# Third chunk's weights split in the opening, values and keys in the scheduler's order, two conditioning vectors summed in the merge, read-back ring dealt anew

## The chip, the cores and the metric

The kernel runs on one core of a Trainium2 chip. The metric is device time in microseconds for one execution of the whole kernel; the kernel before has a median of 1706.3 us over 3 runs (1700.95 to 1707.58). A profile shows the engines apart: PE multiplies matrices, DVE and POOL do elementwise work with two inputs, ACT does activations and copies, and SP issues every DMA, in the order of its own queue. An engine executes its instructions strictly in program order, so one that waits holds all that stand behind it.

## What is computed

One layer of a diffusion transformer on 512 latent tokens and 256 context tokens of width 1024, in single precision. Cut to what matters:

```python
ml = adaln(c, w_mod, b_mod)          # 9 vectors m0..m8 of 1024 for the latents
mc = adaln(c_ctx, w_mod, b_mod)      # and for the context
h  = ffn_sublayer(x,   ml[0:3], ...) # h + 0.5*gate*norm(swiglu(modulate(norm(h), shift, scale)))
hc = ffn_sublayer(ctx, mc[0:3], ...)
xmc = modulate(rms_norm(hc, g), mc[3], mc[4]);  k_c, v_c = split_kv(xmc @ w_in[:, K_OFF:B_OFF])
xm  = modulate(rms_norm(h, g), ml[3], ml[4])
y   = token_mixer(xm @ w_in, k_c, v_c, ...)   # attention branch + short convolution, gated merge, w_o
h   = h + ml[5] * rms_norm(y, g2)
h   = ffn_sublayer(h, ml[6:9], ...)  # second feed-forward block
```

## The kernel before

**How a product is made.** Each matrix operand is split into a high part (a cast to fp32r, `hi`, line 61, on ACT) and a low part (the difference, `lo`, line 67, mostly on DVE). A product is three PE matmuls: high by high, high by low, low by high. A weight block (a unit, 128x1024, 512 KB) comes by one DMA into one of 4 buffers `wraw`, is split into one of 4 buffers each of `whi` and `wlo` (`unit` and `split`, lines 75 to 88), and a buffer is free again when its last reader is through. With `pool_share` 3, every third low part goes to POOL.

**Who sets the order.** Inside `in_order()` (line 91) PE, DVE, ACT and POOL execute in the order in which the code is written. Outside it a scheduler sets the order of each engine, from costs of its own. The DMA queue, SP, is always put in order by the scheduler.

**The stages,** by the time of the profile:
- Opening, to 90 us (line 511): the shift and scale for the first block from `wmod` (`mod_mm` on PE, `mod_col` to DVE, line 345), the normalised input tiles x0 to x7 (`mod_x`, line 365), and the first two of 22 feed-forward chunks on PE, one k after the other (`open_steps`). `mod_t` (line 389) makes differences of a pair of x tiles on POOL, `mod_tp` splits them. The third chunk's weights need sums of their own: `w_pool` (two operations on POOL), `w_dve` (two on DVE), and the splits `w_hi` and `w_lo`.
- Chunks 2 to 21 of gate and up, to 390 us; the hidden rows go to DRAM (`hl_dram`, `hc_dram`).
- Down projection of the latents to 525 us and of the context to 602 us (`down`, line 758), reading the hidden rows back into a ring of 2 buffers `h` in one pool and 2 `h2` in another. Conditioning vectors 2 to 8 are summed on the way: `mod_acc` (line 559) loads a 512 KB block `mraw` of the weights `wmodr` and adds its rows, scaled, into `macc` on DVE (one instruction L572 and seven L575 per half vector); `mod_sum` (line 579) adds over the partitions with two PE matmuls, copies a row out, and sends it through DRAM to a column. Under the context's part of the down projection the latents' `sandwich` (line 1292: rms norm, gate, residual, second norm, modulation into the operand tiles `xs`) runs step by step, one or two steps per chunk (`take(chain, ...)`).
- Values and keys, 602 to 757 us: `values(q, ts)` (line 854) makes a quarter of the values' columns for latent token blocks 2 to 5 and context blocks 0 and 1, `kv_ctx_k(j)` (line 842) a block of the context's keys. The context's `sandwich` has to be through before the context's part. All of it is inside `in_order()`, with the next two units loaded ahead (`next_unit`), with steps of the context's chain between (`take(steps, ...)`), and then with `late_mods`: vectors 6 and 7, which the second feed-forward block needs.
- Attention and convolution to 1083 us, the merge to 1267 us (`pre`, `post`, `onorm`, lines 1119 to 1183: 32 units, eight times gate, convolution, gate and attention projection; `onorm` normalises the attention's output, which `post(0)` needs whole), w_o, the latents' second sandwich, and the second feed-forward block to the end.

Of the kernel before, what the change touches and what calls it, by code (L numbers as in the profile page):

```python
# [16 lines left out]
P = 128  # L17
DM = 1024
ND = 8
NT = 512  # L20
# [19 lines left out]
class Builder:  # L40
    def __init__(self, tc, ctx, io):
        self.tc = tc
        self.nc = tc.nc
        self.ctx = ctx
        self.io = io
        self.n = 0
        self.nu = 0
        self.pool_share = 0
        self.spaced = False

    def pool(self, stack, name, space=None):
# [73 lines left out]
    def rstd_steps(self, pool, psp, tags, sq, T):  # L125
        nc = self.nc
        nb = T // P
        pst = self.t(psp, [P, 512], tags[0], bufs=tags[1])
        for b in range(nb):
            self.mm(pst[:, b:b + 1], sq[0][:, b * P:(b + 1) * P], self.ones[:, 0:1], True, True)  # L130
        if self.spaced:
            yield
        r = self.t(pool, [P, 8], "rstd_s", bufs=2)
        nc.scalar.activation(r[:, :nb], pst[:, :nb], AF.Sqrt, bias=self.eps, scale=1.0 / DM)
        nc.vector.reciprocal(out=r[:, 4:4 + nb], in_=r[:, :nb])
        yield
        if not self.spaced:
            yield
        pb = self.t(psp, [P, 512], tags[0], bufs=tags[1])
        dgs = []  # L140
        for b in range(nb):
            dg = self.t(pool, [P, P], "rstd_d", bufs=4 if self.spaced else 2)
            nc.vector.tensor_scalar(out=dg, in0=self.ident, scalar1=r[:, 4 + b:5 + b],
                                    scalar2=None, op0=ALU.mult)
# [48 lines left out]
    def build(self):  # L193
# [195 lines left out]
        def mod_t(p):  # L389

            x1, x2 = xt[2 * p], xt[2 * p + 1]
            a, b = slice(0, HK), slice(HK, NKEY)
            u = self.t(sp, [P, 2, HK], "sqt", bufs=2)
            v = self.t(sp, [P, 2, HK], "sqt", bufs=2)
            tt = nc.gpsimd.tensor_tensor
            tt(out=u[:, 0, :], in0=x1[:, b], in1=x1[:, a], op=ALU.subtract)
            tt(out=u[:, 1, :], in0=x2[:, b], in1=u[:, 0, :], op=ALU.subtract)
            tt(out=v[:, 0, :], in0=x2[:, b], in1=x1[:, b], op=ALU.subtract)
            tt(out=v[:, 1, :], in0=x2[:, a], in1=u[:, 1, :], op=ALU.subtract)
            tsum[p] = u, v  # L400
# [110 lines left out]
        with self.in_order():  # L511
# [10 lines left out]
            for i in range(4):  # L522
                next(first)
                if i < 3:
                    mod_col(i + 1, rows.pop(i + 1))
                    mod_x(2 * i + 2)
                    mod_x(2 * i + 3)
                mod_tp(i)
                if i < 3:
                    mod_t(i + 1)  # L530
                if i == 2:
                    w_load(2)
                    w_pool(2)
                    w_hi(2, 0)
                    w_lo(2, 0)
                next(first)
                if i < 2:
                    rows[i + 2] = mod_mm(i + 2)
            w_dve(2)
            w_hi(2, 2)  # L540
            w_lo(2, 2)
        ps0 = result(first)
# [14 lines left out]
        accs = {}  # L557

        def mod_acc(pool, m, q, vs, bufs):
# [19 lines left out]
        def mod_sum(pool, psp, tag, pbufs, m, q, v):  # L579

            acc = accs.pop((m, q, v))
            al = self.t(pool, [P, 2, 512], "mraw", F32R, bufs=2)
            self.hi(al[:, 0], acc)
# [45 lines left out]

        def mod_pipe(jobs, pool, tag):  # L630

            when = {}
            for n, (m, q, v) in enumerate(jobs):
                g = mod_sum(pool, psf, tag, 1, m, q, v)
                for part, at in enumerate((0, 2, 4, 6, 10)):
                    when.setdefault(2 * n + at, []).append((-part, g))
# [107 lines left out]
        psf = self.pool(st, "down_ps", PSUM)  # L744
        fp = self.pool(st, "ffn1")
        xs = [slot(d, [P, 2, NT], F32R) for d in range(ND)]
        xhi, xlo = [t[:, 0, :] for t in xs], [t[:, 1, :] for t in xs]
# [4 lines left out]

        def mod_late(jobs):
            for m, vs, bufs in jobs:
                for q in range(2):
                    yield from mod_acc(fp, m, q, vs, bufs)

        def down(src, n, pre, share):
# [26 lines left out]
        pl = [self.t(psf, [P, 512], f"b{d}") for d in range(ND)]  # L785
        mods = mod_late(((4, (0, 1), 4), (5, (0,), None), (8, (0,), None)))
        inorder = ExitStack()
# [20 lines left out]
        sums = mod_pipe([(4, 0, 0), (4, 1, 0), (4, 0, 1), (4, 1, 1), (5, 0, 0), (5, 1, 0), (8, 0, 0),  # L808
                         (8, 1, 0)], fp, "b4")
# [5 lines left out]
        units = (io["wv"][q, hf] for qs in (range(4), range(3)) for q in qs for hf in range(2))  # L815
        units = iter(list(units) + [io["wk"][j] for j in range(NH)])
        self.pool_share = 3
        ready = [self.unit(next(units)) for _ in range(2)]

        def next_unit():  # L820
            src = next(units, None)
            if src is not None:
                ready.append(self.unit(src))
            return ready.pop(0)
# [8 lines left out]
        drain(chain)  # L833
        xc = [self.t(fp, [P, 2, NCX], f"xc{d}", F32R) for d in range(ND)]
        xchi, xclo = [t[:, 0, :] for t in xc], [t[:, 1, :] for t in xc]
        cx = lambda k: (xchi[k], xclo[k])

        chain = self.sandwich(fp, psf, ("b5", 1), yc, sqyc, gp1c, io["ctxT"], smc, mcx[:, 24:32],
                              xchi, xclo, NCX, None, lambda d: ("rctx", 4), share=False)


        def kv_ctx_k(j):
            w = next_unit()
            pk = self.t(psf, [P, 512], f"b{j % 2 * 3}")
# [9 lines left out]
        def values(q, ts):  # L854
# [32 lines left out]
        steps = chain  # L887
        for q in range(3):
            values(q, [2, 3, 4, 5])
            take(steps, 5)  # L890
        drain(chain)
        steps = late_mods()
        values(3, [0, 1, 2, 3, 4, 5])
        take(steps, 6)
        for q in range(3):
            values(q, [0, 1])
            take(steps, 4)
        for j in range(NH):
            kv_ctx_k(j)
            take(steps, 4)  # L900
        drain(steps)
        inorder.close()
        self.spaced = False
        self.pool_share = 0
        st.close()
# [233 lines left out]
        def onorm():  # L1139
            pst = self.t(mps, [P, 512], "pc", bufs=2)  # L1140
            for h in range(NH):
                sq = self.t(mp, [P, NT], "of", bufs=3)
                nc.sync.dma_start(out=sq, in_=o_dram[h])
# [7 lines left out]
                self.mm(pst, eh, sl, False, h == NH - 1)  # L1151
            r = self.t(mp, [P, NT], "of", bufs=3)
            rh = self.t(mp, [P, NT], "osh", F32R, bufs=1)
# [9 lines left out]
            for h in range(NH):  # L1163
# [5 lines left out]
                self.mm(pr, sel, rl, False, True)  # L1169
                of = self.t(mp, [P, NT], "of", bufs=3)  # L1170
                nc.sync.dma_start(out=of, in_=o_dram[h])
# [167 lines left out]
def take(g, n):  # L1339
    for _ in range(n):  # L1340
        next(g, None)
# [105 lines left out]
```

## Time and profile before

| what | us |
|---|---|
| median of 3 runs (1700.95, 1706.3, 1707.58) | 1706.3 |
| the profiled execution's own time | 1708.63 |
| its span, first to last instruction | 1706.5 |
| PE busy | 1598.8 (94%) |
| DVE busy | 1063.6 (62%) |
| ACT busy | 727.7 (43%) |
| POOL busy | 276.3 (16%) |
| idle of PE, longest single waits | 14.1, 10.3, 8.7, 8.1, 6.5, 6.1 |

How to read it: 2.1 us of the profiled execution lie outside the span, and it is 2.3 us above the median. PE is busy nearly all the time, so time can only be won where PE waits, where its clock is below full (the rows give the granted clock as a share of full speed), or by giving it less to do. A row of the waits names the instruction that waited, by engine and line, and the one whose end released it; a row of the windows gives each engine's busy time in a stretch.

### The profile page before, as it was taken

The numbers are of one execution on the slowest core, as the hardware profiler recorded it, in microseconds if no ns is written. First come the engines' busy times: TensorE is split into PE (matmuls) and PEld (weight loads), VectorE is DVE, ScalarE is ACT, GpSimd is POOL, SyncE is SP. The second block draws the span as 40 slices with busy tenths as digits, with TensorE's granted clock in tenths as the row PEclk, the third lists the DMA queues.
The fourth block names the chain that finished last, engine by engine and source line by source line (L and its number), as shares of the span: only waits on it lengthen the run. The fifth ranks groups of instructions, "written<-read, shape, count | busy, mean of one in ns | idle before, by whom it ended". The sixth has DMA issues, their size and how long they took to land. (4 is left out here: it accounts for less than half of the span.)

```text
span 1706.5 us, 23519 instructions
## 1 busy us (share of the span) xinstructions
PE 1598.8 (94%) x8962; PEld 1425.7 (84%) x8962; DVE 1063.6 (62%) x1463; ACT 727.7 (43%) x1139; POOL 276.3 (16%) x208
## 2 busy tenths in 40 slices
PE   5989999998999878599999999999999999999996
PEld 4889999997889878587888888878889998888886
DVE  4598998865656664647877777473347844333345
ACT  4445444442115442244655556452236732222234
POOL 2433444430002430111010000000002100000003
PEclk9989999999999988789999999999999999999998
DMA  9044444447986844868554653643246753233321
GB/s 365 32 154 167 151 158 151 129 157 265 328 310 199 267 130 148 267 213 230 157 155 139 178 145 108 211 152 102 97 134 199 241 150 117 83 111 93 90 81 50
DMA packets 135704, 282.20 MB, mean 165 GB/s; under 512 B 22932, under 2 KB 61972, under 8 KB 135592
## 3 DMA queue, kind: packets, MB, share of 16 engines
q1 hardware_dynamic: 135592, 280.71, 51.2%
q8 instruction: 70, 1.15, 0.3%
q14 instruction: 42, 0.34, 0.1%
HBM read 229.76 MB, written 38.31 MB: 157 GB/s over the span
## 5 line engine op out<-in xcount | busy, mean ns | idle before, releaser
L63 ACT CAST whi<-wraw 128x1024 fp32r<-128x1024 f32 (+1 forms) x264 | 270.9, 1030 | 476.2 <-PE b L781 100.0
L68 DVE TENSOR_TENSOR wlo<-wraw,whi 128x1024 fp32r<-128x1024 f32 (+1 forms) x249 | 331.9, 1335 | 186.1 <-ACT whi L63 181.7
L108 PE MATMUL f<-xs,whi 128*128 128x512 f32 x640 | 201.7, 394 | 0.9 <-DVE rq L926 0.8
L108 PE MATMUL pa<-xs,whi 128*128 128x512 f32 (+1 forms) x704 | 195.8, 361 | 0.7 <-ACT ob L1043 0.5
L781 PE MATMUL b<-h,whi 128*128 128x512 f32 (+1 forms) x704 | 175.3, 341 | 6.5 <-DMA h<-hl_dram 6.5
L108 PEld LDWEIGHTS pa<-xs,whi 128*128 128x128 f32 x704 | 126.0, 189 | 21.0 <-ACT ob L1043 0.7
L781 PEld LDWEIGHTS b<-h,whi 128*128 128x128 f32 x704 | 123.3, 193 | 21.8 <-DMA h<-hl_dram 6.9
L108 PEld LDWEIGHTS f<-xs,whi 128*128 128x128 f32 x640 | 118.1, 188 | 24.6 <-issue 1.7
L108 PE MATMUL pa<-xs,wlo 128*128 128x512 f32 (+1 forms) x352 | 126.9, 361 | 1.5 <-DVE wlo L68 1.5
L108 PE MATMUL f<-xs,wlo 128*128 128x512 f32 x320 | 125.0, 391 | 0.0
L781 PE MATMUL b<-h,wlo 128*128 128x512 f32 (+1 forms) x352 | 119.4, 339 | 0.1
L108 PE MATMUL pb<-xs,whi 128*128 128x512 f32 (+1 forms) x448 | 114.4, 344 | 0.0
L575 DVE SCALAR_TENSOR_TENSOR macc<-mraw,sc,macc 128x512 f32<-128x512 f32 x112 | 95.8, 894 | 10.0 <-DMA mraw<-wmodr 9.4
L108 PEld LDWEIGHTS pb<-xs,whi 128*128 128x128 f32 x448 | 78.1, 189 | 10.0
L172 POOL TENSOR_TENSOR sqacc<-sqacc,sqt 128x256 f32<-128x256 f32 (+1 forms) x20 | 19.0, 950 | 378.4 <-ACT sqt L170 377.0
L108 PE MATMUL pb<-xs,wlo 128*128 128x512 f32 (+1 forms) x224 | 77.1, 344 | 0.0
L108 PEld LDWEIGHTS pa<-xs,wlo 128*128 128x128 f32 x352 | 66.5, 189 | 11.7 <-DVE wlo L68 1.7
L68 POOL TENSOR_TENSOR wlo<-wraw,whi 128x1024 fp32r<-128x1024 f32 x15 | 37.7, 2516 | 231.7 <-ACT whi L63 231.7
L781 PEld LDWEIGHTS b<-h,wlo 128*128 128x128 f32 x352 | 67.7, 192 | 7.4 <-DVE wlo L68 0.3
L1011 ACT ACTIVATE e<-s,mx 128x768 f32<-128x768 f32 x64 | 57.2, 899 | 34.3 <-DVE mx L1007 34.2
L108 PEld LDWEIGHTS f<-xs,wlo 128*128 128x128 f32 x320 | 60.1, 188 | 12.7
L924 POOL TENSOR_TENSOR rot<-rot,cossin 128x512 f32<-128x512 f32 x16 | 22.2, 1390 | 249.7 <-DVE rot L923 231.1
(355 smaller groups left out, 3632.5 us busy)
## 6 DMA issues: line engine op xcount, KB each, us to landing
mraw<-wmodr SPq DMA_DIRECT2D x56, 512.0 KB
wraw<-f2gu SPq DMA_DIRECT2D x56, 512.0 KB
wraw<-f1gu SPq DMA_DIRECT2D x44, 512.0 KB
wraw<-f1d SPq DMA_DIRECT2D x44, 512.0 KB
hl_dram<-h SPq DMA_DIRECT2D x22, 512.0 KB
h<-hl_dram SPq DMA_DIRECT2D x22, 512.0 KB
wraw<-f2d SPq DMA_DIRECT2D x24, 384.0 KB
wm<-wmod SPq DMA_DIRECT2D x16, 512.0 KB
```

The source lines that it names most:

```text
L63: self.nc.scalar.copy(out=out, in_=src)
L68: (eng or self.nc.vector).tensor_tensor(out=out, in0=src, in1=hi.bitcast(F32), op=ALU.subtract)
L108: self.nc.tensor.matmul(out, lhsT=lhsT, rhs=rhs, start=start, stop=stop)
L172: eng.tensor_tensor(out=a, in0=a, in1=s, op=ALU.add)
L575: nc.vector.scalar_tensor_tensor(out=acc, in0=raw[:, k], scalar=s, in1=acc, op0=ALU.mult, op1=ALU.add)
L781: nc.tensor.matmul(o, lhsT=wt[:, c], rhs=x[:, hl], start=start and f + j == 0, stop=f == NF - 1 and j == 2, skip_group_check=True)
L924: nc.gpsimd.tensor_tensor(out=rt, in0=rt, in1=cs[:, 1, :], op=ALU.mult)
L1011: nc.scalar.activation(e[m], ps[:, m * NKEY:(m + 1) * NKEY], AF.Exp, scale=SCALE, bias=mx[:, 2 + m:3 + m], accum_out=mx[:, 4 + m:5 + m])
```

## The change

What it does, part by part:

1. **Opening.** The third chunk's loads, sums and splits stand in round i = 1 of the loop and no longer in round i = 2 and behind the loop. The last `mod_t` (p = 3) runs on DVE and writes over two tiles that are no longer read.
2. **Read-back ring.** Of the hidden rows' buffers, chunk f takes one of pool `h` for f % 4 in (0, 3), and one of `h2` otherwise; before, (0, 1) took `h`.
3. **Context's down projection.** The latents' chain advances 1 and 2 steps in turn; the four later parts of a sum stand at 2, 3, 5, 9 and no longer at 2, 4, 6, 10.
4. **Values and keys.** `in_order()` ends before the context's sandwich, so that the scheduler orders what follows; the sandwich's statistics use PSUM bank b4, and no longer b5; units are loaded where they are used; `late_mods` is gone from here.
5. **Merge.** Vectors 6 and 7 are summed here, 8 steps after each `post(d)`, with one `mraw` buffer (before, two), two `macc` and PSUM bank pd; the ring `of` of `onorm` has 2 buffers, before 3.

The core of the diff:

```diff
-            u = self.t(sp, [P, 2, HK], "sqt", bufs=2)
-            v = self.t(sp, [P, 2, HK], "sqt", bufs=2)
-            tt = nc.gpsimd.tensor_tensor
+            if p < 3:
+                u, v = (self.t(sp, [P, 2, HK], "sqt", bufs=2) for _ in range(2))
+            else:
+                u, v = (self.t(sp, [P, 2, HK], tag) for tag in ("sqacc", "pbs"))
+            tt = (nc.gpsimd if p < 3 else nc.vector).tensor_tensor
...
-                if i == 2:
+                next(first)
+                if i < 2:
+                    rows[i + 2] = mod_mm(i + 2)
+                if i == 1:
                     w_load(2)
                     w_pool(2)
                     w_hi(2, 0)
                     w_lo(2, 0)
-                next(first)
-                if i < 2:
-                    rows[i + 2] = mod_mm(i + 2)
-            w_dve(2)
-            w_hi(2, 2)
-            w_lo(2, 2)
+                    w_dve(2)
+                    w_hi(2, 2)
+                    w_lo(2, 2)
...
-                raw = self.t(pool, [P, 2, 512], "mraw", bufs=2)
+                raw = self.t(pool, [P, 2, 512], "mraw", bufs=n_mraw[0])
...
-                for part, at in enumerate((0, 2, 4, 6, 10)):
+                for part, at in enumerate((0, 2, 3, 5, 9)):
...
-                pool, tag, bufs = (hp, "h", 2) if f % 4 < 2 else (fp, "h2", 2)
+                pool, tag, bufs = (hp, "h", 2) if f % 4 in (0, 3) else (fp, "h2", 2)
...
-            take(chain, 1 if f < 15 else 2)
+            take(chain, 1 + f % 2)
             take(sums, 1)
...
-        ready = [self.unit(next(units)) for _ in range(2)]
...
         drain(sums)
         drain(chain)
+        inorder.close()
...
-        chain = self.sandwich(fp, psf, ("b5", 1), yc, sqyc, gp1c, io["ctxT"], smc, mcx[:, 24:32],
+        chain = self.sandwich(fp, psf, ("b4", 1), yc, sqyc, gp1c, io["ctxT"], smc, mcx[:, 24:32],
...
-                whi, wlo = next_unit()
-                take(steps, 2)
+                whi, wlo = self.unit(io["wv"][q, hf])
...
-        def late_mods():
-            yield from mod_late(((6, (0,), 4), (7, (0,), 4)))
-            yield from mod_pipe([(m, q, 0) for m in (6, 7) for q in range(2)], fp, "b4")
...
-            take(steps, 5)
+            take(chain, 9)
         drain(chain)
...
-                sq = self.t(mp, [P, NT], "of", bufs=3)
+                sq = self.t(mp, [P, NT], "of", bufs=2)
...
+        def merge_mods():
+            for m in (6, 7):
+                yield from mod_late(mp, ((m, (0,), 2),))
+                yield from mod_pipe([(m, 0, 0), (m, 1, 0)], mp, "pd", 2)
+
+        n_mraw[0] = 1
+        mods = merge_mods()
         pre(0)
         onorm()
         pre(1)
         for d in range(ND):
             post(d)
+            take(mods, 8)
             if d + 2 < ND:
                 pre(d + 2)
+        drain(mods)
```

What this moves on the engines, at three places. In the rows, line numbers are each kernel's own, and the numbers behind a name are a buffer's. First DVE in the opening, around the scale and shift of x6 (`mst` and `s_27`, then `xs_50`, which is x6). Before:

```order
L68 TENSOR_TENSOR xs_127_537<-sqt_413,xs_126_536 128x768
L68 TENSOR_TENSOR wm_539<-sqt_414,wm_538 128x768
L355 TENSOR_TENSOR mst_114<-pd_641,vec_66 128x2 x4
L359 SCALAR_TENSOR_TENSOR s_27_115<-mst_114,vec_66 128x2 x2
L369 SCALAR_TENSOR_TENSOR xs_50_144<-xs_50_144,s_27_115,pbs_249 128x512
L68 TENSOR_TENSOR xe_35_123<-xs_50_144,xe_34_122 128x384
```

And now, with the third chunk's sums `s` and low parts `wlx`:

```order
L69 TENSOR_TENSOR xs_127_537<-sqt_413,xs_126_536 128x768
L69 TENSOR_TENSOR wm_539<-sqt_414,wm_538 128x768
L69 TENSOR_TENSOR wlx_614<-wraw_605,whx_613 128x1024
L470 TENSOR_TENSOR s_136_609<-s_136_609,wraw_605 128x512
L471 TENSOR_TENSOR s_137_610<-wraw_605,s_136_609 128x512
L69 TENSOR_TENSOR wlx_620<-s_136_609,whx_619 128x1024
L356 TENSOR_TENSOR mst_114<-pd_659,vec_66 128x2 x4
L360 SCALAR_TENSOR_TENSOR s_27_115<-mst_114,vec_66 128x2 x2
L370 SCALAR_TENSOR_TENSOR xs_50_144<-xs_50_144,s_27_115,pbs_249 128x512
L69 TENSOR_TENSOR xe_35_123<-xs_50_144,xe_34_122 128x384
```

Four instructions stand ahead of x6's scale that stood behind x7's differences; the second, `s_136`, reads what POOL writes.

Second PE at the end of the context's down projection, where the context's statistics begin (`ones` by `sqacc`); `xs` are the latents' operand tiles, and `h` is a chunk of the hidden rows. Before:

```order
L781 MATMUL b_782_4597<-h_5380,whi_5384 128x256 x2
L781 MATMUL b_782_4597<-h_5380,wlo_5385 128x256
L108 MATMUL b_950_5575<-ones_73,sqacc_0_634_3715 128x1 x2
L872 MATMUL b_937_5551<-whi_5491,xs_610_3691 128x256
L872 MATMUL b_937_5551<-wlo_5492,xs_610_3691 128x256
```

And now, with the last rows of the first quarter of the values ahead of the statistics and the first of the second quarter behind:

```order
L869 MATMUL b_932_5540<-whi_5597,xs_617_3698 128x256 x2
L869 MATMUL b_932_5540<-wlo_5598,xs_617_3698 128x256
L869 MATMUL b_932_5540<-whi_5597,xs_617_3698 128x256
L109 MATMUL b_949_5675<-ones_73,sqacc_0_634_3715 128x1 x2
L869 MATMUL b_960_5716<-whi_5720,xs_610_3691 128x256
L869 MATMUL b_960_5716<-wlo_5721,xs_610_3691 128x256
```

The statistics stood directly behind the down projection and ahead of all values; now a whole quarter of the latents' values stands between.

Third DVE in the merge, while `onorm` squares the attention's output (`osl` is the low part of a head's square) and the branches' weights are split (`wlo`). Before:

```order
L68 TENSOR_TENSOR osl_10104<-of_10101,osh_10103 128x512
L68 TENSOR_TENSOR osl_10113<-of_10110,osh_10112 128x512
L68 TENSOR_TENSOR osl_10122<-of_10119,osh_10121 128x512
L1125 TENSOR_TENSOR cv_10308<-sb_10275,pb_10283 128x512
L68 TENSOR_TENSOR wlo_10414<-wraw_10411,whi_10413 128x1024
L68 TENSOR_TENSOR osl_10131<-of_10128,osh_10130 128x512
```

And now:

```order
L69 TENSOR_TENSOR osl_10017<-of_10014,osh_10016 128x512
L580 SCALAR_TENSOR_TENSOR macc_10273<-mraw_10278,sc_80,macc_10273 128x512
L69 TENSOR_TENSOR wlo_10359<-wraw_10356,whi_10358 128x1024
L69 TENSOR_TENSOR osl_10026<-of_10023,osh_10025 128x512
L580 SCALAR_TENSOR_TENSOR macc_10273<-mraw_10282,sc_80,macc_10273 128x512
L69 TENSOR_TENSOR osl_10035<-of_10032,osh_10034 128x512
L580 SCALAR_TENSOR_TENSOR macc_10273<-mraw_10282,sc_80,macc_10273 128x512
L69 TENSOR_TENSOR wlo_10392<-wraw_10389,whi_10391 128x1024
```

Sums of vector 6 stand between the low parts of the heads and of the weights. Over this stretch, up to the low part of the last head's normalised output, DVE has 16 of these sums, and PE has 299 matmuls of the merge ahead of the first `post`, where before it had 251.

More of the change, by code (lines that the diff above doesn't have):

```diff
@@ L49, in __init__ @@
         self.spaced = False
+        self.n_dg = 2
     def pool(self, stack, name, space=None):
@@ L141, in rstd_steps @@
         for b in range(nb):
-            dg = self.t(pool, [P, P], "rstd_d", bufs=4 if self.spaced else 2)
+            dg = self.t(pool, [P, P], "rstd_d", bufs=self.n_dg)
             nc.vector.tensor_scalar(out=dg, in0=self.ident, scalar1=r[:, 4 + b:5 + b],
@@ L557, in build @@
         accs = {}
+        n_mraw = [2]
         def mod_acc(pool, m, q, vs, bufs):
@@ L581, in mod_sum @@
             acc = accs.pop((m, q, v))
-            al = self.t(pool, [P, 2, 512], "mraw", F32R, bufs=2)
+            al = self.t(pool, [P, 2, 512], "mraw", F32R, bufs=n_mraw[0])
             self.hi(al[:, 0], acc)
@@ L628, in mod_early, with mod_pipe @@
                     ends.extend(sums)
-        def mod_pipe(jobs, pool, tag):
+        def mod_pipe(jobs, pool, tag, bufs):
             when = {}
             for n, (m, q, v) in enumerate(jobs):
-                g = mod_sum(pool, psf, tag, 1, m, q, v)
-                for part, at in enumerate((0, 2, 4, 6, 10)):
+                g = mod_sum(pool, psf, tag, bufs, m, q, v)
+                for part, at in enumerate((0, 2, 3, 5, 9)):
                     when.setdefault(2 * n + at, []).append((-part, g))
@@ L745, in build @@
         fp = self.pool(st, "ffn1")
+        self.n_dg = 4
         xs = [slot(d, [P, 2, NT], F32R) for d in range(ND)]
@@ L751, in build, with mod_late @@
         sqyc, sqyl = self.sqsum(fp, NCX), self.sqsum(fp, NT)
-        def mod_late(jobs):
+        def mod_late(pool, jobs):
             for m, vs, bufs in jobs:
                 for q in range(2):
-                    yield from mod_acc(fp, m, q, vs, bufs)
+                    yield from mod_acc(pool, m, q, vs, bufs)
         def down(src, n, pre, share):
@@ L785, in build @@
         pl = [self.t(psf, [P, 512], f"b{d}") for d in range(ND)]
-        mods = mod_late(((4, (0, 1), 4), (5, (0,), None), (8, (0,), None)))
+        mods = mod_late(fp, ((4, (0, 1), 4), (5, (0,), None), (8, (0,), None)))
         inorder = ExitStack()
@@ L808, in build @@
         sums = mod_pipe([(4, 0, 0), (4, 1, 0), (4, 0, 1), (4, 1, 1), (5, 0, 0), (5, 1, 0), (8, 0, 0),
-                         (8, 1, 0)], fp, "b4")
+                         (8, 1, 0)], fp, "b4", 1)
         self.spaced = True
@@ L812, in build @@
         for f, _ in enumerate(part):
-            take(chain, 1 if f < 15 else 2)
+            take(chain, 1 + f % 2)
             take(sums, 1)
-        units = (io["wv"][q, hf] for qs in (range(4), range(3)) for q in qs for hf in range(2))
-        units = iter(list(units) + [io["wk"][j] for j in range(NH)])
         self.pool_share = 3
-        ready = [self.unit(next(units)) for _ in range(2)]
[L820 to L824, printed above, removed]
         for d in range(ND):
@@ L833, in build @@
         drain(chain)
+        inorder.close()
+        self.spaced = False
         xc = [self.t(fp, [P, 2, NCX], f"xc{d}", F32R) for d in range(ND)]
@@ L836, in build @@
         cx = lambda k: (xchi[k], xclo[k])
-        chain = self.sandwich(fp, psf, ("b5", 1), yc, sqyc, gp1c, io["ctxT"], smc, mcx[:, 24:32],
+        chain = self.sandwich(fp, psf, ("b4", 1), yc, sqyc, gp1c, io["ctxT"], smc, mcx[:, 24:32],
                               xchi, xclo, NCX, None, lambda d: ("rctx", 4), share=False)
         def kv_ctx_k(j):
-            w = next_unit()
+            w = self.unit(io["wk"][j])
             pk = self.t(psf, [P, 512], f"b{j % 2 * 3}")
@@ L881, in values @@
                               .rearrange("t p n -> p t n"), vh[:, hl])
-        def late_mods():
-            yield from mod_late(((6, (0,), 4), (7, (0,), 4)))
-            yield from mod_pipe([(m, q, 0) for m in (6, 7) for q in range(2)], fp, "b4")
-        steps = chain
         for q in range(3):
             values(q, [2, 3, 4, 5])
-            take(steps, 5)
+            take(chain, 9)
         drain(chain)
-        steps = late_mods()
         values(3, [0, 1, 2, 3, 4, 5])
-        take(steps, 6)
         for q in range(3):
             values(q, [0, 1])
-            take(steps, 4)
         for j in range(NH):
             kv_ctx_k(j)
[L900 to L904, printed above, removed]
+        self.pool_share, self.n_dg = 0, 2
         st.close()
@@ L1151, in onorm @@
                 self.mm(pst, eh, sl, False, h == NH - 1)
-            r = self.t(mp, [P, NT], "of", bufs=3)
+            r = self.t(mp, [P, NT], "of", bufs=2)
             rh = self.t(mp, [P, NT], "osh", F32R, bufs=1)
@@ L1169, in onorm @@
                 self.mm(pr, sel, rl, False, True)
-                of = self.t(mp, [P, NT], "of", bufs=3)
+                of = self.t(mp, [P, NT], "of", bufs=2)
                 nc.sync.dma_start(out=of, in_=o_dram[h])
```

## The prediction

> **What bounds the kernel now.** I read the page first, for the engine that sets the time:
>
> ```profile
> span 1706.5 us, 23519 instructions
> PE 1598.8 (94%) x8962; PEld 1425.7 (84%) x8962; DVE 1063.6 (62%) x1463; ACT 727.7 (43%) x1139; POOL 276.3 (16%) x208
> ```
>
> PE is idle for 1706.5 - 1598.8 = 107.7 us. The waits of PE say where; I kept the rows that lie in stages that the change touches (the engine, the line and tile that waited, what released it, the total, how often, the longest):
>
> ```profile
> PE b L872 <- DVE wlo L68: 11.3, 2, 6.1
> PE b L108 <- DVE tmp L178: 10.3, 1, 10.3
> PE b L108 <- ACT mraw L63: 8.7, 1, 8.7
> PE pa L663 <- ACT g L645: 8.1, 1, 8.1
> PE b L108 <- ACT macc L591: 6.6, 4, 4.4
> PE b L781 <- DMA h<-hl_dram: 6.5, 1, 6.5
> PE b L108 <- DVE sqacc L172: 4.7, 2, 2.9
> PE b L108 <- DVE rstd_d L143: 2.8, 1, 2.8
> ```
>
> Then the windows, to see how much each stage loses and at which clock. The columns are the stretch, its length, each engine's busy time with its instructions, PE's granted clock, the DMA engines' busy share and GB/s:
>
> ```profile
> 602.00:641.00 39.00, 26.52 (x200) 26.34 (x200) 23.37 (x43) 15.79 (x32) 12.46 (x11) 0.82 0.39 129
> 641.00:680.00 39.00, 33.97 (x252) 33.53 (x253) 17.82 (x31) 10.35 (x17) 2.94 (x1) 0.87 0.38 130
> 680.00:719.00 39.00, 24.44 (x166) 23.83 (x164) 23.89 (x30) 8.02 (x10) 4.76 (x2) 0.82 0.85 276
> 719.00:757.00 38.00, 28.80 (x181) 26.30 (x182) 19.93 (x29) 16.17 (x25) 4.77 (x2) 0.78 0.60 181
> 622.00:638.00 16.00, 16.00 (x136) 16.00 (x135) 10.44 (x17) 5.29 (x11) 6.39 (x6) 1.00 0.40 132
> 641.00:649.00 8.00, 4.65 (x24) 4.62 (x25) 3.77 (x7) 2.14 (x3) 0.00 (x0) 0.57 0.60 195
> 1083.00:1142.00 59.00, 58.36 (x252) 45.84 (x250) 31.60 (x47) 29.57 (x42) 0.00 (x0) 1.00 0.69 234
> ```
>
> Values and keys, 602 to 757 us, are the worst stage: in 155 us PE is busy for 26.52 + 33.97 + 24.44 + 28.80 = 113.7 us, so 41.3 us idle, and it is busy at a clock of 0.78 to 0.87, while the quiet stretch 622 to 638 has 1.00. The merge's first 59 us lose nothing.
>
> **Values and keys.** What has to be done there is in the groups of PE between 602 and 757 us (shape and count, then busy and mean ns):
>
> ```profile
> L872 PE MATMUL b<-whi,xs 128*128 128x256 f32 x256 | 51.7, 298 | 0.0
> L872 PE MATMUL b<-wlo,xs 128*128 128x256 f32 x128 | 37.9, 296 | 0.0
> L872 PE MATMUL b<-whi,xc 128*128 128x256 f32 x128 | 28.9, 317 | 1.7 <-ACT xc L183 1.1 <-DVE xc L184 0.6
> L108 PE MATMUL b<-xc,whi 128*128 128x256 f32 x128 | 26.4, 307 | 0.3 <-DVE kch L68 0.3
> L872 PE MATMUL b<-wlo,xc 128*128 128x256 f32 x64 | 20.6, 322 | 11.3 <-DVE wlo L68 11.3
> L108 PE MATMUL b<-xc,wlo 128*128 128x256 f32 x64 | 19.5, 305 | 0.0
> L108 PE MATMUL b<-mraw,ones_r 128*128 128x512 f32 x8 | 4.5, 632 | 12.2 <-ACT mraw L63 8.7 <-ACT macc L591 2.3 <-DVE mraw L68 1.2
> ```
>
> Matmuls overlap, so their mean is not their price; the price is the quiet stretch's, 16.00 / 136 = 0.118 us each, and I take 0.12 because a record or two overlap the stretch's ends. There are 256 + 128 + 128 + 128 + 64 + 64 = 768, so 92 us. The two statistics and their spreading are some 16 small matmuls, which I put at 4 us, and what remains at the edges at 1. The stage's work is thus 97 us of its 155; 58 us are loss, and the eight matmuls of the sums leave with it.
>
> How much of the loss goes? The 10.3 us stand at 612 us: PE has nothing but the context's statistics to do there, and their bank b5 is still read by the latents' last modulation on DVE. The change puts a whole quarter of the values, 96 matmuls or 11.5 us, ahead of the statistics, and takes another bank, so PE has work from the first moment; its operands `xs` are then due at the end of the down projection, and the chain that makes them runs at one and a half steps per chunk, so I count them ready. The 11.3 and the 8.7 us are both due to vectors 6 and 7, for DVE is held by their loads, with the weights' low parts queued behind:
>
> ```profile
> DVE macc L575 <- DMA mraw<-wmodr: 9.4, 8, 2.1
> DVE macc L572 <- DMA mraw<-wmodr: 3.6, 2, 1.9
> ```
>
> They leave the stage altogether. What is late next is the context's own chain: two statistics and two spreadings, of which this trace shows waits of 2.9 and 2.8 us. In the new order a quarter stands in front of each statistic, and some 13 matmuls (1.6 us) between it and its spreading. I bound what is left by 0, if all is covered, and by four waits of 2.9 us or 11.6 us, and take 4, nearer the covered end because each chain step now has 11.5 us of PE's work ahead of it. Weights come in 22 units of 512 KB in 97 us, 119 GB/s, and the values go out beside them; the stage moved 276 GB/s in its third window, so I count them as hidden; were they not, see the second rival. The stage takes 97 + 4 = 101 us: **54 us won** (58 to 43, the latter with 11.6 us of waits and their clock).
>
> The clock belongs to that price. Between 641 and 649 us two waits of 2.9 and 2.8 us went with a clock of 0.57. [...]
>
> **The context's down projection.** Of the 6.6 us for `macc` most is one wait of 4.4 us, in which ACT came late with a sum's row copy because it stood behind a weight's load:
>
> ```profile
> 564.26 1.04 ACT L63 CAST whi<-wraw 128x1024 fp32r<-128x1024 f32 x1 [8.94 <-DMA wraw<-f1d]
> 565.75 0.56 ACT L591 COPY macc<-b 1x512 f32<-1x512 f32 x1
> ```
>
> The load itself was issued late, since SP's queue stood behind a write of the latents' chain. In the new spacing each row copy stands one chunk sooner, and the chain's steps lie otherwise, so that a write holds another load, or none in need. I expect 3 us to go, between 0 (the same load is held again) and 7 (all of the 6.6 goes).
>
> **The read-back ring.** The first read of the latents' down projection waits 6.5 us for its hidden rows. The second buffer comes from the other pool, so that its load need not wait for the last spill. The queue at that place (start and length):
>
> ```profile
> 398.34 1.52 SPq L73 DMA_DIRECT2D h<-hl_dram  x3
> ```
>
> The load moves up by a place or two among issues of some 0.5 us, and shares the DMA engines with fewer others: **2 us** of the 6.5, between 0 and 6.5.
>
> **The opening.** These are the rows of DVE, POOL, ACT and PE on which it turns (start, duration):
>
> ```profile
> 67.95 1.46 DVE L369 SCALAR_TENSOR_TENSOR xs<-xs,s,pbs 128x512 f32<-128x512 f32 x1
> 71.72 0.55 DVE L68 TENSOR_TENSOR h<-xs,h 128x384 fp32r<-128x384 f32 x1
> 77.70 2.03 DVE L68 TENSOR_TENSOR wlx<-wraw,whx 128x1024 fp32r<-128x1024 f32 x1
> 86.42 0.68 DVE L467 TENSOR_TENSOR s<-s,wraw 128x512 f32<-128x512 f32 x1
> 67.86 1.01 POOL L399 TENSOR_TENSOR sqt<-xs,sqt 128x384 f32<-128x384 f32 x1
> 82.48 1.27 POOL L461 TENSOR_TENSOR s<-wraw 128x512 f32<-128x512 f32 x1
> 89.50 0.60 ACT L645 ACTIVATE g<-pa 128x512 f32<-128x512 f32 x1
> 72.10 0.34 PE L156 MATMUL pa<-xe,whi 128*128 128x384 f32 x1
> 90.14 1.01 PE L663 MATMUL pa<-xe,whx 128*128 128x384 f32 x2 [8.12 <-ACT g L645]
> ```
>
> x6 is scaled from 67.95, its last low part ends at 72.27, and PE takes it at 72.10: just in time. Now POOL's sum stands behind the third `mod_t`, which ends at 68.87, and ends at 68.87 + 1.27 = 70.1; DVE waits for it, then makes two sums (0.68 each, 71.5), then, after a cast, a low part of 2.0, and so reaches x6 near 74. x6 comes some 6 us later than before: a new stall of 6 us ahead of k = 6, and about 2 us of slow clock behind it. The end of the opening's matmuls moves from 82.0 (90.14 - 8.12) to 90. For that the 8.1 us ahead of the third chunk go, since its splits are done; only a Silu of 0.6 us and its table are left, and PE starts that chunk at about 91 instead of 90.1, but no longer at the half speed that followed the 8.1 us, worth 2.5. **1.5 us won**; if x6 is late by 2 us only, 6 are won, and if by 8, with twice the slow clock, 3 are lost.
>
> **The merge.** Here the vectors arrive again: 32 sums on DVE, 16 loads, 8 matmuls.
>
> ```profile
> L575 DVE SCALAR_TENSOR_TENSOR macc<-mraw,sc,macc 128x512 f32<-128x512 f32 x112 | 95.8, 894 | 10.0 <-DMA mraw<-wmodr 9.4
> 1104.00:1146.00 42.00, 41.82 (x179) 32.23 (x178) 30.02 (x40) 25.26 (x38) 0.00 (x0) 1.00 0.52 165
> ```
>
> The matmuls cost 8 x 58.36 / 252 = 1.9 us. The tight place is `post(0)`, which needs all heads normalised; from 1104 to 1146 us DVE is busy for 30.0 of 42 us with that. Sixteen of the sums now lie in this stretch, 16 x 0.894 = 14.3 us, so 44.3; with a single `mraw` buffer each of the eight loads may hold DVE, by (9.4 + 3.6) / 10 = 1.3 us each as in the rows above, 10.4 us: 54.7 us. For this the scheduler puts 48 more matmuls ahead of `post(0)`, 48 x 0.23 = 11.1 us, so that DVE has 53.1 us. A stall of 2 us by this sum, between 0 and 16 (if the idle time of before can't be filled); I take 4, since SP's loads for `onorm` queue behind those of `mraw`. Sums 17 to 32 lie where DVE has ample idle time. **6 us lost** (2 to 18).
>
> [...]
>
> Between keys and attention a load may come later than now; I count 1 us (0 to 3).
>
> **The sum.** 54 + 3 + 2 + 1.5 - 6 - 1 = 53.5 us. The profiled execution took 1708.6 us, of which 2.1 lie outside its span, and it stands 2.3 us above the median. 1708.6 - 53.5 = 1655, against the median's 1706.3: **1653 us**.
>
> **The rivals.** *The wait moves along with the vectors.* In values and keys the sums cost PE 11.3 + 8.7 us and about 3 of the other sums' waits, with perhaps 7 us of clock, 30 us in all. In the merge there is half the buffering and the same single queue, so the same may happen. Against it: PE has four units in hand there, and the windows show a clock of 1.00. It gives 1653 + 30 - 6 = 1677. *Weights late.* Two units were loaded ahead by hand; the scheduler may load them where they are needed. If each of 22 units costs 1 us, 1675; for it speaks a DMA share of 0.85 in the third window, against it that this window held most of the 16 loads that leave. *Nothing left over.* All chains covered and no stall at `post(0)`: values and keys at 97, the merge at 2, 1645 or less. *No change.* The stage is held by DMA, whatever the order: near 1700; but its first half runs at shares of 0.39 and 0.38 and loses 17.5 us all the same. *Slower.* SP holds a weight behind each `mraw` load, the load waits for DVE, and PE waits for the weight: at half of the 11.3 us for two such waits, 5.65 us, for all 16 loads, 90 us; with the merge at 92 instead of 6 the total is 1653 + 86 = 1739. It is slower than before from 3.7 us per load (59 us in all). Against it: four `wraw` buffers cover several loads.
>
> **How the numbers follow.** The likeliest case, 1653, has a chance of 0.62; the wait that moves along 0.16; late weights 0.10; nothing left over 0.07; slower 0.03; no change 0.02. The bounds of the unknown terms, all good or all bad, would reach from 1632 to 1686; rarely all at once, so for 8 in 10 the range is 1636 to 1680, which holds the likeliest case and most of the next two. A measurement of this kernel tells about 0.5%, 8.5 us, from no change. Faster by more than that: 0.62 + 0.16 + 0.10 + 0.07 = 0.95; within it 0.02; slower 0.03.
>
> **What would show it.** Right: PE's wait on `tmp` L178 gone, values and keys 97 to 112 us long at a clock near 1.00, no `mraw` in their waits; a new wait near 72 us for x6, and no 8 us for `g`; at `post(0)` a wait of a few us for a head's `o`. Wrong: waits on `wlo` or on weights between the quarters; waits on `macc` loads in the merge that add up to 20 us or more; a stage of values and keys above 125 us.

## The result, and the profile after

The changed kernel has a median of 1662.94 us over 4 runs (1660.94 to 1668.42), the kernel before 1705.51 us over 4. The ratio is 0.9759, with a 95% interval of 0.9727 to 0.9791: faster by 2.4%, some 43 us, where 53.5 were forecast. The page's first lines after:

```profile
span 1662.3 us, 23526 instructions
PE 1590.7 (96%) x8962; PEld 1418.7 (85%) x8962; DVE 1061.0 (64%) x1467; ACT 728.4 (44%) x1139; POOL 274.6 (17%) x204
```

The work is the same, 8962 matmuls; PE's idle time fell from 107.7 to 71.6 us. Its waits after (same columns as before; rows of the stages that were changed):

```profile
PE pa L157 <- ACT xe L64: 10.5, 2, 7.0
PE b L787 <- ACT whi L64: 4.6, 1, 4.6
PE b L787 <- DMA h<-hl_dram: 4.3, 1, 4.3
PE b L109 <- DVE sqacc L173: 4.0, 2, 2.0
PE pc L109 <- DVE of L1157: 2.9, 2, 1.7
PE pd L109 <- ACT mraw L64: 2.0, 1, 2.0
PE b L109 <- DVE ml L608: 0.9, 1, 0.9
```

The rows of `tmp`, `wlo` and `mraw` in values and keys, and that of `g`, are gone. New are 7.0 us for x6 (`xe`; the other 3.5 us of its row were there before), and two rows in the merge (`of`, `mraw` to bank pd). The windows of values and keys, and of the merge to and from the first `post`:

```profile
604.00:702.00 98.00, 94.82 (x789) 94.06 (x788) 54.41 (x89) 42.65 (x72) 23.12 (x15) 1.00 0.67 215
1028.00:1104.00 76.00, 70.32 (x298) 55.07 (x298) 45.55 (x65) 31.56 (x44) 0.00 (x0) 0.98 0.76 258
1104.00:1222.00 118.00, 118.00 (x513) 97.22 (x514) 59.87 (x64) 37.02 (x49) 9.89 (x7) 0.98 0.40 125
```

Values and keys have a clock of 1.00 and 3.2 us of idle time; the merge has 5.7 us of idle time ahead of the first `post`, where it had 0.6. From the first and last matmuls of each stage in the two traces:

| stage | before, us | after, us | change | forecast |
|---|---|---|---|---|
| opening and chunks, to the first down projection | 392.5 | 392.7 | +0.2 | -1.5 |
| down projection, latents | 136.5 | 134.8 | -1.7 | -2 |
| down projection, context | 72.8 | 76.6 | +3.8 | -3 |
| values and keys | 154.3 | 97.6 | -56.7 | -54 |
| attention | 327.0 | 326.3 | -0.7 | +1 |
| merge | 183.7 | 193.8 | +10.1 | +6 |
| from w_o to the end | 439.7 | 440.5 | +0.8 | 0 |

The sum is -44.2 us, the difference of the two spans.

### The profile page after: what moved, and what is told of

It reads as the page before. It is cut to its first block, busy times and chain, and to the rows that moved or that the text cites. A ratio compares the mean times of both kernels' runs of the same rounds, so it can differ in the third digit from the quotient of the medians.

```text
span 1662.3 us, 23526 instructions
## 1 busy us (share of the span) xinstructions
PE 1590.7 (96%) x8962; PEld 1418.7 (85%) x8962; DVE 1061.0 (64%) x1467; ACT 728.4 (44%) x1139; POOL 274.6 (17%) x204
## 5 line engine op out<-in xcount | busy, mean ns | idle before, releaser
L69 DVE TENSOR_TENSOR wlo<-wraw,whi 128x1024 fp32r<-128x1024 f32 (+1 forms) x249 | 327.5, 1317 | 181.8 <-ACT whi L64 175.4
L787 PE MATMUL b<-h,whi 128*128 128x512 f32 (+1 forms) x704 | 178.7, 345 | 9.0 <-ACT whi L64 4.6
```

Source lines behind the costliest of these rows:

```text
L69: (eng or self.nc.vector).tensor_tensor(out=out, in0=src, in1=hi.bitcast(F32), op=ALU.subtract)
L787: nc.tensor.matmul(o, lhsT=wt[:, c], rhs=x[:, hl], start=start and f + j == 0, stop=f == NF - 1 and j == 2, skip_group_check=True)
```

## The experiments

Times of stages are from each kernel's own trace, one execution each, between the same matmuls as in the table. The changed kernel is the base unless another is named.

### Values and keys: the vectors or the order

**Vectors 6 and 7 back among values and keys, in the scheduler's order.**

```diff
+        steps = late_mods()
         values(3, [0, 1, 2, 3, 4, 5])
+        take(steps, 10)
...
-            take(mods, 8)
...
-                sq = self.t(mp, [P, NT], "of", bufs=2)
+                sq = self.t(mp, [P, NT], "of", bufs=3)
```

> Vectors 6 and 7 are summed among values and keys again, with two mraw buffers, but in the scheduler's order; the merge is as before, its ring of 3 too. Theory A (the vectors' loads hold DVE and ACT wherever they are): values and keys take 97.8 + 20 to 27 us, so about 120, the merge falls back from 193.4 to 183 us, the total is about 1663 + 23 - 10 = 1676. Theory B (the order written by hand was at fault, the scheduler hides the vectors): values and keys stay under 106 us (97.8, 2 us of matmuls and some), the total is about 1659.

Measured: 1670.73 us (ratio to before 0.9796, 0.9772 to 0.9820). Values and keys took 113.1 us, the merge 183.8. The window and the largest wait there:

```profile
601.00:714.40 113.40, 100.64 (x796) 98.75 (x794) 83.12 (x129) 46.83 (x80) 26.06 (x15) 0.95 0.79 256
```

```profile
PE b L109 <- ACT macc L596: 4.9, 1, 4.9
```

Neither theory's number: with the vectors back the stage is 15.5 us longer, and the merge 10 us shorter. The scheduler hides part of them, no wait on `wlo` comes back, but a sum's row copy still stops PE for 4.9 us, and the clock over the window is 0.95, where the changed kernel's stage has 1.00.

**Values and keys inside the hand-written order, the vectors in the merge.**

```diff
         drain(chain)
-        inorder.close()
         self.spaced = False
...
+        inorder.close()
         self.pool_share, self.n_dg = 0, 2
```

> The changed kernel with values and keys inside the hand-written order again; the vectors stay in the merge. Theory A (the vectors were the loss): values and keys take 97.8 us plus four waits of the context's statistics and spreading of up to 2.9 us and their clock, 100 to 112 us, the total 1665 to 1677. Theory B (the hand-written order was the loss): values and keys take over 125 us, the total is over 1690.

Measured: 1773.10 us (ratio 1.0387, 1.0361 to 1.0412), slower than the kernel before; values and keys took 203.0 us. Window, then waits:

```profile
604.00:807.00 203.00, 128.97 (x786) 121.37 (x785) 54.15 (x86) 44.43 (x72) 22.39 (x15) 0.74 0.31 102
```

```profile
PE b L868 <- ACT whi L64: 38.0, 7, 9.8
PE b L109 <- ACT whi L64: 11.5, 8, 1.6
```

By its number theory B, but the rows give another cause than B: PE waits for the high part of each unit's weights. Written in the order of use, a unit's split stands on ACT behind the casts of the values of the group before (`vch`), which wait for PE: ACT is idle for 51.1 us ahead of five of them. The old code had covered this by two units split ahead, which the change removed. So I put the lead back.

**The same with two units split ahead.**

```diff
-                whi, wlo = self.unit(io["wv"][q, hf])
+                whi, wlo = next_unit()
...
-            w = self.unit(io["wk"][j])
+            w = next_unit()
```

> As the kernel with values and keys inside the hand-written order and the vectors in the merge (203.0 us for values and keys), but two units are split ahead again, as before the change. Theory (in the hand-written order a unit's split stands behind work that waits for PE, and only the lead covers it; the vectors were the rest of the loss): values and keys fall to 100 to 112 us, the total to 1665 to 1677. Rival (the steps of the context's chain stand badly in the hand-written order, lead or not): values and keys stay over 125 us.

Measured: 1673.84 us (ratio 0.9812, 0.9793 to 0.9832), values and keys 106.8 us, as the theory has it:

```profile
605.00:712.00 107.00, 97.93 (x786) 97.65 (x787) 54.83 (x87) 43.27 (x71) 22.83 (x15) 0.95 0.60 193
```

**The same, and the vectors back as well** (the edits of the first and the third experiment, with the takes of before: 2 per unit, then 6, 4 and 4, on `late_mods`; the merge as before).

> The hand-written order with the lead of two units (106.8 us for values and keys), and vectors 6 and 7 summed there again at the steps of before; the merge has none and its reads' ring is three. Theory (in the hand-written order the vectors' sums stand on DVE ahead of the weights' low parts and wait for their loads): values and keys take 130 to 145 us, 24 to 38 more than without the vectors, where the scheduler's order pays 15.5 for them, with waits of PE on wlo and mraw of 15 us or more; the merge takes 183 us, the total is about 1690. Rival (the vectors cost the same in either order, and before the change it was the place of the statistics and of the chain's steps): values and keys take 120 to 125 us.

Measured: 1699.29 us in one run, above the 1690 expected (some 2 of the 9 us lie in the opening, see below); values and keys 141.9 us, as expected. Window and waits:

```profile
607.00:749.00 142.00, 108.30 (x793) 105.02 (x792) 82.48 (x126) 47.08 (x78) 23.24 (x15) 0.87 0.65 204
```

```profile
PE b L879 <- DVE wlo L69: 13.5, 3, 6.7
PE b L109 <- ACT mraw L64: 7.6, 1, 7.6
```

These are the old waits. The vectors cost 141.9 - 106.8 = 35.1 us in the hand-written order and 15.5 in the scheduler's.

**The bank alone, from both sides.** In the changed kernel the context's statistics go back to b5; in the kernel before they go to b4.

```diff
-        chain = self.sandwich(fp, psf, ("b4", 1), yc, sqyc, gp1c, io["ctxT"], smc, mcx[:, 24:32],
+        chain = self.sandwich(fp, psf, ("b5", 1), yc, sqyc, gp1c, io["ctxT"], smc, mcx[:, 24:32],
```

> The changed kernel with the context's statistics in the old bank b5. Theory (the 10.3 us went because a quarter of the values now stands ahead of the statistics): values and keys stay at 97 to 99 us. Rival (the bank did it): a wait of PE on tmp of more than 2 us is back.

> The kernel before with the context's statistics in bank b4 and nothing else changed. Theory (at the end of the down projection PE has only the statistics to do, which need the context's eight tiles copied and squared anyway, to 610.4 us): PE still waits 8 to 9 us there, for sqacc instead of tmp, and values and keys take 152 to 154 us. Rival (the bank did it): the wait falls under 4 us and values and keys take under 148 us.

Measured: with b5 values and keys took 97.7 us (1660.22 in one run) and no wait on `tmp` came back. In the kernel before, b4 left this wait (1703.14 us in one run, values and keys 151.1, just under the theory's 152):

```profile
609.18 1.02 PE L108 MATMUL b<-ones,sqacc 128*128 128x1 f32 x4 [8.61 <-DVE sqacc L172]
```

So 8.6 of the 10.3 us were not the bank's: the statistics stood first, and what they sum was not ready. The bank was worth 3.2 us at most in the kernel before, less than a microsecond in the new order.

### The merge

**No sum before `onorm` is through with its buffers, and two `mraw` buffers.**

```diff
-                accs[m, q, v] = (self.t(pool, [P, 512], "macc", bufs=bufs) if bufs else
+                accs[m, q, v] = (self.t(pool, [P, 512], ("osh", "osl")[q]) if pool is not fb and pool is not fp else
+                                 self.t(pool, [P, 512], "macc", bufs=bufs) if bufs else
...
-        n_mraw[0] = 1
+        n_mraw[0] = 2
```

> The changed kernel with the two accumulators of the merge in the buffers of onorm's high and low parts, so that no sum can begin before onorm is through with them; the room this leaves goes to a second mraw buffer. Theory (sums ahead of post(0) on DVE delay the heads): the waits of 1.3, 1.7 and 2.0 us and the half clock of 7 us around post(0) go, the merge falls from 193.4 to about 186 us, the total is about 1655. Rival (the ring of two buffers for the heads' reads delays them): the waits stay within 1 us of these, the total stays at 1663.

Measured: 1663.25 us (ratio 0.9749, 0.9733 to 0.9765), the merge 197.2 us. PE's waits on `of` stayed, 3.3 us in two. My theory fell, and the rival was left. In the changed kernel DVE itself waits for a head's read just ahead of PE's wait, by its timeline and PE's:

```profile
1097.11 0.75 DVE L1157 SCALAR_TENSOR_TENSOR of<-of,sg,pc 128x512 f32<-128x512 f32 x1 [1.18 <-DMA of<-o_dram]
```

```profile
1097.91 0.50 PE L109 MATMUL pc<-osh,sel 128*128 128x512 f32 x1 [1.28 <-DVE of L1157]
```

**The late sums with one `mraw` buffer, and the room given to a third `of` buffer.**

```diff
-                sq = self.t(mp, [P, NT], "of", bufs=2)
+                sq = self.t(mp, [P, NT], "of", bufs=3)
```

> The changed kernel with the merge's accumulators in the buffers of onorm's high and low parts and one mraw buffer, and the room given to a third buffer for the heads' reads (of). Theory (the reads' ring of two makes DVE and PE wait for a head's load between the heads): the waits of PE on of, 2.9 to 3.3 us, go, the first post starts within 71 us of the merge's start where it took 76.4, and with the half clock behind it the merge takes 185 to 190 us, the total about 1657. Rival (the sums or the order itself): a wait of 3 us on of stays, the total within 3 us of 1663.

Measured: **1653.61 us** (ratio 0.9700, 0.9684 to 0.9716), faster than both kernels. The merge took 187.9 us, and no wait on `of` is left. Its windows to and from the first `post`:

```profile
1024.00:1083.00 59.00, 58.78 (x253) 46.59 (x254) 32.64 (x48) 30.25 (x43) 0.00 (x0) 1.00 0.70 243
1083.00:1212.00 129.00, 126.84 (x560) 104.34 (x560) 72.40 (x82) 38.31 (x51) 10.08 (x7) 1.00 0.49 155
```

The first `post` comes after 59 us and some 250 matmuls, as before the change. What is left of the vectors' price is one wait of 2.2 us and their matmuls. The median is 9.3 us under the changed kernel's; of that the merge explains 5.9. Most of the rest is clock in stages whose code is the same: the context's down projection took 72.9 us here and 76.6 in the changed kernel, with a clock of 0.98 against 0.92 from 529 to 604 us (see the last section).

**Vectors 6 and 7 left out.**

```diff
-            take(mods, 8)
...
+        nc.vector.memset(ml[:, 48:64], 0.0)
```

> The changed kernel without vectors 6 and 7: their loads, sums and columns are left out, and zeros stand in their place; the reads' ring stays at two. If the vectors make the whole of the merge's loss, the merge takes 183 to 185 us as before, the first post starts 59 to 61 us after the merge's start, and the total is about 1653. If the ring of two makes part of it, a wait of PE on of of 1 to 3 us stays and the merge takes 186 to 190 us.

Measured: 1660.63 us in one run; the merge took 190.6 us, and PE still waits:

```profile
PE pc L109 <- DVE of L1160: 3.6, 2, 1.9
```

So the ring of two costs the merge 190.6 - 183.7 = 6.9 us by itself, and the vectors the other 3.2 of 10.1; with a ring of three they cost 187.9 - 183.7 = 4.2, which leaves 5.9 to the ring. The ring also moves the first `post`: without any vector PE still has 296 matmuls of the merge ahead of it, as the changed kernel has 298, where the kernel before has 250.

### The opening, the ring and the spacing

**The opening and the read-back ring of before,** undone as in the diff above.

> The changed kernel with the opening and the read-back ring of before. Theory (the opening's new stall for x6 costs what the old wait for g cost): the wait of 8 us for g is back, that of 7 us for x6 is gone, and the third chunk and the first read-back stand within 1.5 us of the changed kernel's 90.9 and 392.7. The ring alone: the first read-back waits 6.5 us again where it waits 4.3, so the total is 1 to 3 us longer, about 1665. Rival: the opening brings 3 us or more by itself, and the read-back starts at 396 or later.

Measured: 1662.52 us in one run. The old waits are back:

```profile
PE pa L665 <- ACT g L647: 8.2, 1, 8.2
PE b L784 <- DMA h<-hl_dram: 5.9, 1, 5.9
```

The third chunk starts at 92.5 and the down projection at 394.9 us, 2.2 later than after the change. But the same opening reached it at 392.5 in the kernel before. The clock tells why: from 37.5 to 60 us, ahead of all that the new opening moves, it is 0.81 in this run (156 matmuls) and 1.00 in the kernel before (183) and in the changed one (196). The run with the vectors back in the hand-written order has the new opening and 0.82 there, and it too reaches the down projection at 394.9 us. At 1.00 the old opening reaches it at 392.5 and, with bank b4, 391.8, the new one at 392.5 to 393.4 in nine kernels. So the new opening wins nothing. The ring is worth 1.6 us (5.9 against 4.3).

**x6 ahead of the third chunk's sums** (base: the kernel with late sums and three `of` buffers).

```diff
+                if i == 2:
+                    w_pool(2)
+                    w_hi(2, 0)
+                    w_lo(2, 0)
                 mod_tp(i)
+                if i == 2:
+                    w_dve(2)
+                    w_hi(2, 2)
+                    w_lo(2, 2)
                 if i < 3:
                     mod_t(i + 1)
...
                 if i == 1:
                     w_load(2)
-                    w_pool(2)
...
-                    w_lo(2, 2)
```

> The kernel with late sums and the reads' ring of three (1653.6 us), and in the opening the third chunk's sums and splits stand behind x7's and no longer ahead of x6's: only the loads stay in round 1. Theory (the new wait of 7.0 us for x6 is made by the four DVE instructions and POOL's sum ahead of it, and the splits have time until the eighth k ends): the wait for x6 is under 1 us, no wait of 8 us for g comes back, the third chunk starts at 83 to 86 us where it started at 90.5, and the total is 1645 to 1650. Rival (the last pair's differences on DVE are then late and the wait moves to the third chunk's second product): the chunk starts early but waits 3 to 6 us, and the total is 1651 to 1655.

Measured: 1657.17 us (1653.62 to 1659.62; ratio 0.9708, 0.9685 to 0.9732), no better: the third chunk starts at 90.4 us, as in its base (90.5). The wait for x6 fell to 1.1 us, but PE waits for `g` again, now for another reason. ACT's timeline, then PE's:

```profile
86.58 0.83 ACT L64 CAST xs<-sqacc 128x768 fp32r<-128x768 f32 x1 [4.83 <-DVE pbs L401]
88.48 1.28 ACT L653 ACT_TABLE_LOAD   x1 [0.34 <-DVE xs L69]
89.78 0.60 ACT L653 ACTIVATE g<-pa 128x512 f32<-128x512 f32 x1
```

```profile
90.43 1.01 PE L671 MATMUL pa<-xe,whx 128*128 128x384 f32 x2 [7.60 <-ACT g L653]
```

The Silu stands on ACT behind the casts of the last pair's differences, and these wait for DVE to 86.5 us. Neither of my two cases: the wait went back to the chunk's first product. A version that lets the Silu pass was not tried.

**The old pace and spacing in the context's down projection.**

```diff
-            take(chain, 1 + f % 2)
+            take(chain, 1 if f < 15 else 2)
...
-                for part, at in enumerate((0, 2, 3, 5, 9)):
+                for part, at in enumerate((0, 2, 4, 6, 10)):
```

> The changed kernel with the old pace of the latents' chain (1 step per chunk, 2 from chunk 15) and the old spacing of the sums. Theory (the new spacing made the context's down projection worse, from 72.8 to 76.5 us): it takes 73 us again. Rival (the wait for a weight's load of 4.4 to 4.6 us is there in both, and what differs is only which waits fall into a stretch of half clock): a wait of 4 to 5 us stays, and the length moves by the clock alone. If the faster chain is what lets the values start at once, a wait of 2 to 10 us on xs appears at their start; if the order alone does it, none.

Measured: 1667.82 us in one run; the stage took 74.9 us, values and keys 102.2. Two of its waits:

```profile
PE b L109 <- ACT macc L596: 3.5, 1, 3.5
PE b L869 <- ACT xs L64: 2.2, 1, 2.2
```

The theory's 73 us did not come; its clock is half for 6.8 us twice, as in the changed kernel (the first time 0.50 from 527.7 to 534.5 us in both), so the 1.7 us by which the stage is shorter than the 76.6 there are not clock. The wait on the row copy is back and that on `whi` gone: one and the same late weight's load, met by another instruction. SP issues it behind a write of the latents' chain in both spacings, at 559.76 us in the changed kernel and at 559.84 in the kernel before. Eleven us into the values PE waits 2.2 us for `xs`; the new pace and spacing together are worth 102.2 - 97.6 = 4.6 us in values and keys.

## Why the prediction was right, and where it was off

The time lies in the range, and the mechanism of the main term was the forecast one; three of the terms were wrong in sign or size. The spans differ by 44.2 us, 9.3 less than forecast: 6.8 of that lie in the context's down projection and 4.1 in the merge. (The outer bounds of the unknown terms add up to 1631 and 1687, and not to 1632 and 1686.)

- **Values and keys, 54 forecast, 56.7 measured.** The stage's work was put at 97 us; it took 97.6 with all that waited. One row of its groups after shows the price, busy 48.5 us where it was 51.7 for the same 256 matmuls:

```profile
L869 PE MATMUL b<-whi,xs 128*128 128x256 f32 x256 | 48.5, 284 | 0.0
```

  Waits of 0.9 and 2.0 us were left of the four (4 us were put down). The 2.0 us cost no clock here (1.00 over the stage); the last section has an idle time of that length that did. The parts of the 56.7 us, one after the other: 154.3 to 141.9 for the place of the statistics and of the chain's steps, 141.9 to 106.8 for the vectors, 106.8 to 97.6 for the scheduler's order. Other orders of the steps would share it out otherwise: with the vectors there the scheduler's order is worth about 141.9 - 113.1 = 28.8 us. The prediction gave that order no term of its own. I had put down the 10.3 us to bank b5 as much as to the order; it was the order.
- **Context's down projection, 3 won forecast, 3.8 lost.** The step that failed is "in the new spacing ... a write holds another load, or none in need". The wait on `macc` went, and a wait on `whi` of 4.6 us took its place: the late load was still needed. PE's waits behind the statistics add up to 5.3 us, as good as the 5.5 of before. The 3.8 us lost are clock: it was half for 6.8 us behind the latents' statistics (0.50 from 527.7 to 534.5 us), where the kernel before lost none (1.00 from 525.5 to 535 us), and for 6.8 us behind the wait on `whi` (0.50 from 565.2 to 572.0 us), where before it was half for 3.4 us (0.50 from 566.25 to 569.66 us). This comes in some executions only: with this code the stage took 72.6 to 73.4 us in five of the kernels (those of the first, the b5, the late-sums, the three-buffer and the old-opening experiments; from 529 to 604 us their clock was 0.95 to 0.98) and 76.4 to 77.4 in six others, the changed kernel among them (0.91 or 0.92 there in five of the six). So the new spacing wins nothing over the 72.8 us of before even where the clock holds.
- **Read-back ring, 2 forecast, 1.7 measured;** the wait fell from 6.5 to 4.3 us.
- **Opening, 1.5 won forecast, 0.2 lost.** The mechanism was as worked out, DVE behind POOL's sum at 70.2 us, x6 scaled at 74.9 where "near 74" was forecast, the stall 7.0 where 6 was:

```profile
70.23 0.69 DVE L470 TENSOR_TENSOR s<-s,wraw 128x512 f32<-128x512 f32 x1 [4.10 <-POOL s L464]
74.90 1.72 DVE L370 SCALAR_TENSOR_TENSOR xs<-xs,s,pbs 128x512 f32<-128x512 f32 x1
```

  The third chunk started at 90.9 us, forecast 91. What was won in clock behind it (0.50 from 90.1 to 95.2 us in the kernel before, 1.00 now) was mostly spent on two new waits of 0.7 us.
- **Merge, 6 lost forecast, 10.1 measured.** The step that failed is the choice of the tight resource: I summed DVE's work and the `mraw` loads, and gave the ring of `onorm`'s reads, 3 buffers to 2, no price of its own. It was 5.9 to 6.9 of the 10.1 us, and it also made the 48 matmuls more ahead of the first `post`, which I had put down to the vectors. The sums and their loads made no stall there: without them PE waits on `of` as long (3.6 us against 2.9), and moving them behind `onorm` did not shorten the merge (197.2 us).
- **The rivals.** "The wait moves along with the vectors" did not come in that form: no `wlo` waits in the merge, and 10 us, not 30. Weights were not late. The rival that the lead of two units mattered was right for the hand-written order alone, where its loss cost 96 us (203.0 against 106.8); in the scheduler's order it was not needed.

## What to carry to other kernels

An order written by hand and the loads ahead that go with it are one thing: take away the lead alone and each split queues behind work that waits for PE; take away both and the scheduler may do better. When work is moved to another stage to make room, price what was made smaller for it there as carefully as the work itself: the ring that lost a buffer cost more than the moved work did (5.9 to 6.9 us against 3.2 to 4.2). And a stall that goes because its instruction moved may only be met by the next one in line, if the transfer behind it is as late as before.

## What the runs showed of the hardware

A short idle time cost more in clock than in time in one kernel, and no clock in another. In the changed kernel and in the one with late sums and three `of` buffers the code to this point is the same, and PE idles about 2.0 us for the latents' statistics. The windows around it, of the changed kernel:

```profile
525.50:527.70 2.20, 0.23 (x3) 0.22 (x2) 1.80 (x4) 1.62 (x3) 0.00 (x0) 0.99 0.32 106
527.70:534.50 6.80, 6.80 (x33) 6.80 (x33) 6.52 (x9) 5.48 (x8) 2.47 (x1) 0.50 0.51 161
```

And of the other:

```profile
525.20:527.40 2.20, 0.23 (x3) 0.16 (x2) 1.83 (x3) 1.57 (x3) 0.00 (x0) 1.00 0.41 117
527.40:534.20 6.80, 6.73 (x55) 6.52 (x56) 6.49 (x9) 6.37 (x8) 2.81 (x2) 1.00 0.57 179
```

In one the clock is 0.50 for the next 6.8 us, and PE gets 33 matmuls done, in the other it is 1.00, and 55.

The clock records of two traces, of the kernel before and of the changed kernel, have 21 stretches at half clock. In each trace they start at whole multiples of 3.41 us from one another, to 0.1 us, and all but the last one of each last 3.4, 6.8, 10.2 or 13.7 us. I laid PE's busy time over these steps of 3.41 us, from 40 us on to 15 us before the end, and looked at the steps at full clock. All 13 in which PE was busy for less than 0.44 of the step were followed by half clock, so were the 4 with 0.48 to 0.53, and none of the 899 with 0.56 or more was. The latents' statistics are an example of both. In the changed kernel the wait of 2.0 us, 525.5 to 527.5, lies within the step that begins at 524.25 us; PE is busy for 0.42 of it, and half clock follows. In the kernel before the wait of 1.8 us, 527.2 to 529.1, is parted at 528.69 us; PE is busy for 0.57 of the one step and 0.87 of the next, and the clock stays at 1.00. Where the steps lie in the kernel with late sums and three `of` buffers is not shown here.
